# Nine double pairs of a SwiGLU feed-forward layer: a second split for product 3, a ring of four weights, four raw places, and moved X sums

## The chip, the cores and the metric

The kernel runs on one core of one Trainium2 chip. The metric is the device time of one execution in microseconds, the median of several runs. Smaller is better. A second number is the span of one profiled execution, from its first to its last recorded instruction, which the profile's shares refer to.

## The reference, cut to what matters

One decoder layer for 1032 tokens (a prompt of 1024 and 8 samples), in float32 with D_MODEL = 1024 and D_FF = 2816:

```python
def swiglu(x, wi, wo):
    g, u = jnp.split(x @ wi, 2, axis=-1)
    return (jax.nn.silu(g) * u) @ wo
...
    x = layer_norm(ALPHA * x + 0.5 * swiglu(x, ffn1_wi, ffn1_wo), ln_g[0], ln_b[0])
    z = x @ w_in + b_in
...
    x = layer_norm(ALPHA * x + mix, ln_g[1], ln_b[1])
    x = layer_norm(ALPHA * x + 0.5 * swiglu(x, ffn2_wi, ffn2_wo), ln_g[2], ln_b[2])
```

Between the two feed-forward layers stand an mLSTM branch and a short convolution branch, which the change does not touch. What it touches is `x @ wi` of both feed-forward layers: a product of the 1032 x 1024 activations with the gate and the up weights, 1024 x 2816 each.

## The kernel before, in words

**Precision.** Every float32 operand is split into a high part (a rounded copy in the format that the PE multiplies, "fp32r") and a low part (the difference). ACT makes the high part with a cast, DVE the low part with a subtraction. `product` (L490) issues three matmuls for each 128-row chunk: high weight by high X (L493), high weight by low X (L494), low weight by high X (L495).

**Pairs.** The 2816 gate columns and the 2816 up columns are cut into 11 pairs of 256, numbered 0 to 10. A pair's gate product (half k=0) and its up product (half k=1) are each a 2 x 2 block product of weights (two halves of K, two column blocks of 128) and X (two halves of K, two halves of 516 tokens). It is done with seven half products instead of eight, the scheme of Strassen and Winograd, numbered 0 to 6. A half product is done for two token pieces of 256 and 260 columns (`BN`), four K chunks and three matmuls each: 12 matmuls for a piece. Pair 0 is done plainly in `plain`, pair 1 with `hidden` and `pair` (L499), pairs 2 to 10 with `pair2` (L545), once gate and up together. These nine are the **double pairs**.

**The second split.** Product 1 of the gate half and product 1 of the up half multiply the same X block, so that together they are again a 2 x 2 block product: two weights, two halves of their K, two token pieces. `pair2` does them with seven quarter products of six matmuls, each 260 columns wide: 42 matmuls in place of 48. Their seven X operands `XQ` are made once for each feed-forward layer by `quarters` (L245), from the X blocks b11, b21, b12, b22 of product 1: ten sums on POOL, six on DVE, eight splits into high and low, and two small copies. The generator is advanced by the `beside` list: `pair` pops an entry after each step. The weights for quarters come from `wquarter` (L277): it packs two quarter weights into one slot.

**Weights.** For each pair and half, `wi_raw` (L677) issues two loads of 512 KB from the SP queue into two of three raw places (`raws`, 2 x 512 rows by 256 columns, named a30, a31, a32 in the first feed-forward layer), in rotation. `wcomb` (L306) forms the seven weights of a half: sums s1 and s2 on DVE, s3 and s4 on POOL, in `raw` tiles (a pool of 3), and then each weight's high and low part in a slot of the **ring**: nine tiles w0 to w5, e0, e1, cd, less one that `quarters` occupies (`qslots[2]`, w5), eight in all. A slot is free again when the last matmul on its weight is done.

**Results.** A half's products gather in PSUM tiles: `mm` (4 buffers), `aux` (3) and `pn` (1). ACT copies intermediate states into the snapshot tile (`sreg`, views `SN`), DVE adds the later ones to them; the gate passes through Silu on ACT and is multiplied with the up half on DVE (L569, L631). `spill` (L658) then forms the sums that the second weight matrix needs (L669, L671 on DVE, two on POOL) and stores them to `hsum` by nine transfers on the SP queue. The four `tmp` buffers, shared by `quarters`, by the up half and by `spill`, are free when their store has landed.

**What sets the order.** A scheduler lists each engine's instructions, by the order of the code, by data, by free buffers, and by `tc.high_priority()` and `tc.issue_after(...)`. Each engine then runs its list in order, so that an instruction that waits holds back all that stand behind it on the same engine. After the last double pair come the segments, the products with `wo`.

Each feed-forward layer runs one after the other: the first from the start to about 640 us, with the double pairs from 106 us, the second from about 1820 us, with its double pairs from about 1926 us.

## Time and profile before

| | |
|---|---|
| runs, us | 2669.59, 2673.85, 2673.53 |
| median, us | 2673.53 |
| profiled execution, its own time, us | 2669.52 |
| its span, us | 2667.2 |
| granted TensorE clock, mean | 0.997 |
| PE busy, us | 2622.7 |
| DVE busy, us | 1936.0 |
| ACT busy, us | 1293.1 |
| POOL busy, us | 696.0 |

The profile's page gives, for one profiled execution, the busy time of each engine, the chain of work that ended last, and groups of instructions. The trace behind it answers closer questions: busy time in stretches of the span (windows), what an engine waited for (waits), and single instructions with start and duration (timeline). An instruction of the timeline has its start in us, its duration, engine, line and operands; in brackets stands the idle time ahead of it and what ended it. A matmul's recorded duration overlaps that of the next, so its price is the distance from one start to the next.

### The profile page before, as it was taken

What the parts mean: (1) busy time and instruction counts of PE and PEld (TensorE: products, weight loads), DVE (VectorE), ACT (ScalarE), POOL (GpSimd) and SP (SyncE); (2) the same over time, 40 slices, a digit from 0 to 9 for tenths busy, and PEclk for the clock granted to TensorE, in tenths of its full rate; (3) what the DMA queues carried; (4) which work ended last, traced back from release to release, by engine and by line L of the source; (5) the groups of instructions that cost most, each with busy time, mean ns of one, the idle gap of its engine ahead of it and who ended that gap; (6) DMA issues with size and microseconds to landing.
All of it is one profiled execution on the core that took longest, in us unless ns stands there. A gap on an engine that the chain in (4) does not pass through costs nothing.

```text
span 2667.2 us, 56283 instructions
## 1 busy us (share of the span) xinstructions
PE 2622.7 (98%) x21660; PEld 2581.9 (97%) x21660; DVE 1936.0 (73%) x4272; ACT 1293.1 (48%) x2873; POOL 696.0 (26%) x705
## 2 busy tenths in 40 slices
PE   9999999999999999999999999999999999999998
PEld 9999999999999999999999999999999999999888
DVE  6867667987886656555555678668966666988787
ACT  5544446433654445446656555425544444543451
POOL 2422221112421111111110336323432222111454
PEclk9999999999999999999999999999999999999999
DMA  6232335532233434236667676812233324643211
GB/s 209 84 112 88 108 104 194 188 118 73 86 112 104 124 100 128 80 98 197 193 194 249 215 238 218 273 54 86 94 108 107 105 88 131 224 149 111 79 49 56
DMA packets 311924, 355.14 MB, mean 133 GB/s; under 512 B 28536, under 2 KB 246344, under 8 KB 311656
## 3 DMA queue, kind: packets, MB, share of 16 engines
q1 hardware_dynamic: 289336, 330.30, 39.0%
q10 hardware_dynamic: 22320, 21.26, 2.7%
q8 instruction: 169, 2.77, 0.4%
q14 instruction: 99, 0.81, 0.1%
HBM read 246.09 MB, written 105.42 MB: 132 GB/s over the span
## 4 chain that ended last, share of the span: by engine, by line
PE 87%; DVE 7%; DMA 2%; issue 2%; ACT 1%; POOL 1%; SPq 0%; DVEq 0%; ACTq 0%; POOLq 0%
PE mm L493 15%; PE mm L495 15%; PE mm L494 15%; PE mm L172 6%; PE aux L493 6%; PE mm L174 6%; PE mm L173 6%; PE aux L494 5%; PE aux L495 5%; PE pn L174 1%; PE pn L172 1%; PE pn L173 1%; DVE a L756 1%; DVE a L216 1%; PE pn L493 1%
## 5 line engine op out<-in xcount | busy, mean ns | idle before, releaser
L493 PE MATMUL mm<-a,w 128*128 128x260 f32 (+1 forms) x2511 | 712.8, 284 | 3.7 <-DVE a L779 3.1
L494 PE MATMUL mm<-a,w 128*128 128x260 f32 (+1 forms) x2511 | 706.5, 282 | 0.1
L495 PE MATMUL mm<-a,w 128*128 128x260 f32 (+1 forms) x2511 | 706.1, 282 | 0.0
L493 PEld LDWEIGHTS mm<-a,w 128*128 128x128 f32 x2511 | 473.7, 189 | 13.3 <-issue 8.0
L494 PEld LDWEIGHTS mm<-a,w 128*128 128x128 f32 x2511 | 474.0, 189 | 0.3 <-DVE a L216 0.3
L495 PEld LDWEIGHTS mm<-a,w 128*128 128x128 f32 x2511 | 473.2, 189 | 0.9 <-issue 0.8
L336 POOL TENSOR_TENSOR raw<-a,raw 128x512 f32<-128x512 f32 (+2 forms) x98 | 130.2, 1328 | 1026.7 <-DVE w L316 449.2
L316 DVE TENSOR_TENSOR w<-raw,w 128x512 fp32r<-128x512 f32 (+2 forms) x273 | 186.6, 684 | 126.9 <-ACT w L315 125.7
L493 PE MATMUL aux<-a,w 128*128 128x256 f32 (+1 forms) x760 | 215.4, 283 | 0.9 <-DVE a L515 0.7
L494 PE MATMUL aux<-a,w 128*128 128x256 f32 (+1 forms) x760 | 214.2, 282 | 1.8 <-DVE a L216 1.8
L315 ACT CAST w<-raw 128x512 fp32r<-128x512 f32 (+2 forms) x273 | 161.1, 591 | 111.6 <-PE mm L495 63.6
L174 PE MATMUL mm<-a,w 128*128 128x256 f32 (+4 forms) x758 | 214.6, 286 | 0.0
L495 PE MATMUL aux<-a,w 128*128 128x256 f32 (+1 forms) x760 | 213.6, 281 | 0.0
L172 PE MATMUL mm<-a,w 128*128 128x260 f32 (+3 forms) x712 | 204.6, 288 | 3.4 <-ACT w L1488 2.0
L173 PE MATMUL mm<-a,w 128*128 128x260 f32 (+3 forms) x712 | 202.7, 286 | 0.0
L493 PE MATMUL mm<-a,e 128*128 128x260 f32 (+1 forms) x629 | 178.7, 284 | 1.8 <-ACT sreg L511 0.8
L494 PE MATMUL mm<-a,e 128*128 128x260 f32 (+1 forms) x629 | 177.1, 281 | 0.0
L495 PE MATMUL mm<-a,e 128*128 128x260 f32 (+1 forms) x629 | 176.9, 281 | 0.0
L315 ACT CAST w<-a 128x512 fp32r<-128x512 f32 (+2 forms) x176 | 102.8, 586 | 147.9 <-PE mm L495 56.0
L326 POOL TENSOR_TENSOR raw<-a 128x512 f32<-128x512 f32 (+2 forms) x98 | 124.6, 1271 | 174.4 <-DVE w L316 80.0
L493 PEld LDWEIGHTS aux<-a,w 128*128 128x128 f32 x760 | 143.1, 188 | 3.5 <-issue 2.1
L494 PEld LDWEIGHTS aux<-a,w 128*128 128x128 f32 x760 | 143.1, 188 | 2.2 <-DVE a L216 2.2
(574 smaller groups left out, 7946.4 us busy)
## 6 DMA issues: line engine op xcount, KB each, us to landing
a<-in_ffn_wi_dram SPq DMA_DIRECT2D x80, 512.0 KB
a<-in_w_in_dram SPq DMA_DIRECT2D x68, 512.0 KB
a<-hsum SPq DMA_DIRECT2D x119, 258.0 KB
hsum<-a SPq DMA_DIRECT2D x68, 258.0 KB
a<-in_ffn_wo_dram SPq DMA_DIRECT2D x40, 384.0 KB
a<-in_state_C_dram ACTq DMA_DIRECT2D x32, 256.0 KB
out_dram<-a ACTq DMA_DIRECT2D x32, 256.0 KB
raw<-in_w_b_dram SPq DMA_DIRECT2D x32, 256.0 KB
```

The lines of the kernel that those rows point to most:

```text
L172: T.matmul(ps, wh, xh, start=(i == 0), stop=False)
L173: T.matmul(ps, wh, xl, start=False, stop=False)
L174: last = T.matmul(ps, wl, xh, start=False, stop=(i == n - 1))
L216: order_["lo"] = V.tensor_tensor(dst[1], src, F_(dst[0]), op=OP.subtract).ins
L315: S.copy(hi, src)
L316: V.tensor_tensor(lo, src, F_(hi), op=OP.subtract)
L326: G.tensor_tensor(s3, a11, a21, op=OP.subtract)
L336: G.tensor_tensor(s4, a12, s2, op=OP.subtract)
L493: T.matmul(ps, wh, xh, start=start and kp == 0, stop=False, skip_group_check=True)
L494: T.matmul(ps, wh, xl, start=False, stop=False, skip_group_check=True)
L495: T.matmul(ps, wl, xh, start=False, stop=stop and kp == len(xs) - 1, skip_group_check=True)
L756: V.tensor_tensor(lo, F_(lo), F_(hi), op=OP.subtract)
```

## The change

It has five parts.

1. **Product 3 is done by the second split too**, from pair 3 on (`LEVEL2 = {2: 1, 3: 3}`: product 1 from pair 2, as before, product 3 from pair 3). That is 42 matmuls in place of 48 in eight double pairs of each feed-forward layer. The seven quarter weights of product 3 come from the other half of the weights' columns; each pair makes seven more quarter weights, and two weights of 512 columns less.
2. **The X operands of product 3** are made by a second run of `quarters`, beside the first half of pair 3, into the tiles w4, e0 and e1. The X sums of product 1, which before stood beside the up half of pair 1, now stand beside the first half of pair 2.
3. **The ring has four slots** from pair 3 on: w0 to w3. At pair 2 it has eight. cd becomes a raw place.
4. **Four raw places**: each of a pair's four loads has its own place (`raws[:3] + ["cd"]`) in place of three in rotation. Some sums are now written in place into a raw tile (s3 over a21, s4 over s2).
5. **`pair2` is written anew** around `wcomb2`, a generator that yields the gate weights and then the up weights, in the order in which they are used: `first` and `second` are the steps of the gate and the up half, and the quarters of product 1 and then those of product 3 stand between the steps of the second half. Their results are added to the gate and up states with high priority.

In the core of the diff below, the lines left out are the old forms of `wquarter`, `wcomb` and `pair2`, and steps of `first` and `second` that read as those of the old `step`.

```diff
...
+    def use_ring(slots):
+        set_ring([i for i in from_ring() if i in slots])
...
-    def quarters(XS, slots):
-
-        (b11, b21), (b12, b22) = XS[0][9], XS[1][9]
+    def quarters(XS, j, slots):
...
+    def wcomb2(ra, rb, js):
...
+        def blocks(r):
+            return [u[:, :, i:i + 128] for u in r for i in (0, 128)]
+
+        def sums(r):
+            a11, a21, a12, a22 = blocks(r)
+            s1, s2 = k4(fresh()), k4(fresh())
+            V.tensor_tensor(s1, a21, a22, op=OP.add)
+            G.tensor_tensor(a21, a11, a21, op=OP.subtract)
+            V.tensor_tensor(s2, s1, a11, op=OP.subtract)
+            return s1, s2, a21
+
+        def last(r, s2):
+            G.tensor_tensor(s2, blocks(r)[2], s2, op=OP.subtract)
+            return s2
+
+        def quarter(i):
+            a11, a12, a21, a22 = (u[1][:, k:k + 2, i:i + 128] for u in (ra, rb) for k in (0, 2))
+            out = {1: put2(a12)}
+            yield out
+            out[0] = put2(a11)
+            yield
+            s1, s2 = (t.rearrange("p (k n) -> p k n", n=128) for t in fresh().rearrange("p (a m) -> a p m", a=2))
+            V.tensor_tensor(s1, a21, a22, op=OP.add)
+            V.tensor_tensor(s2, s1, a11, op=OP.subtract)
+            out[4] = put2(s1)
+            out[2] = put2(s2)
+            s3, s4 = (t.rearrange("p (k n) -> p k n", n=128) for t in fresh().rearrange("p (a m) -> a p m", a=2))
+            G.tensor_tensor(s3, a11, a21, op=OP.subtract)
+            G.tensor_tensor(s4, a12, s2, op=OP.subtract)
+            yield
+            out[3] = put2(a22)
+            out[5] = put2(s3)
+            yield
+            out[6] = put2(s4)
+            yield
+
+        wa, wb = {}, {}
+        s1, s2, s3 = sums(ra)
+        wa[0] = put(blocks(ra)[0])
+        wa[2] = put(s2)
+        if 3 not in js:
+            wa[3] = put(blocks(ra)[3])
+        wa[4] = put(s1)
+        s4 = last(ra, s2)
+        wa[5] = put(s3)
+        wa[6] = put(s4)
+        yield wa
+        wb[0] = put(blocks(rb)[0])
+        q = quarter(0)
+        wb[1] = next(q)
+        next(q)
+        next(q)
+        s1, s2, s3 = sums(rb)
+        wb[2] = put(s2)
+        next(q)
+        next(q)
+        if 3 in js:
+            q = quarter(128)
+            wb[3] = next(q)
+            next(q)
+            wb[4] = put(s1)
+            next(q)
+            next(q)
+            next(q)
+        else:
+            half.clear()
+            wb[3] = put(blocks(rb)[3])
+            wb[4] = put(s1)
+        s4 = last(rb, s2)
+        wb[5] = put(s3)
+        wb[6] = put(s4)
+        yield wb
+
...
+    def pair2(ws, XS, XQ, da, fa, fb):
 
...
-        for k, w in enumerate(ws):
-            P = {}
+        def quarter(ps, w, j, start, stop, x):
+            product(ps, w[j], [(x[j][:, 2 * k], x[j][:, 2 * k + 1]) for k in range(2)], start, stop)
+
+        def part(ps, d):
+            return ps[:, 0:d.shape[1]]
+
+        def add(d, ps, op=OP.add):
+            with tc.high_priority():
+                V.tensor_tensor(d, d, part(ps, d), op=op)
+
+        def minus(d, ps):
+            with tc.high_priority():
+                V.scalar_tensor_tensor(d, d, -1.0, part(ps, d), op0=OP.mult, op1=OP.add)
+
+        P = {}
+
...
+        add(g0, F)
+        add(g0, A)
+        add(u1, E)
+        fa(0, 0)
+        second(2, 0, w)
+        quarter(A, q, 2, False, False, x)
+        G_ = aux(BM)
+        quarter(G_, q, 3, True, True, x)
+        add(g1, A)
+        add(u0, G_, OP.subtract)
+        second(2, 1, w)
+        quarter(A, q, 5, False, True, x)
+        quarter(E, q, 6, False, True, x)
+        add(u0, A)
+        add(u1, A)
+        add(g1, E)
+        fa(0, 1)
+        for s, u in ((0, u0), (1, u1)):
+            fb(0, s, u)
+        if 3 in XQ:
+            q, x = w[3], XQ[3]
+            h0, h1 = (bs(da[1], s, BLK4) for s in range(2))
+            v0, v1 = (SN["v"][2][s] for s in range(2))
+            F, A = aux(BM), aux(BM)
+            quarter(F, q, 1, True, True, x)
+            quarter(A, q, 0, True, False, x)
+            add(h0, F, OP.subtract)
+            add(h0, A, OP.subtract)
+            fa(1, 0)
+            second(4, 0, w)
+            E = psp.tile([128, 512], F32, name="pn", tag="pn", bufs=1)[:, :BM]
+            quarter(E, q, 4, True, False, x)
+            S.copy(v1, E)
+            quarter(A, q, 2, False, False, x)
+            add(h1, A, OP.subtract)
+            G_ = aux(BM)
+            quarter(G_, q, 3, True, True, x)
+            S.copy(v0, part(G_, v0))
+            second(4, 1, w)
...
+    LEVEL2 = {2: 1, 3: 3}
...
         def wi_raw(p, k):
             i = 4 * p + 2 * k
-            return wraw(wi, k * FF + p * 256, [raws[(i + q + 2) % 3] for q in range(2)])
+            return wraw(wi, k * FF + p * 256, [(raws[:3] + ["cd"])[2 * k + q] if p > 2 else raws[(i + q + 2) % 3]
+                                               for q in range(2)])
 
...
-        set_ring([i for i in r if i != qslots[2]])
         wr = wi_raw(1, 0)
         with tc.issue_after(order_["entered"]) if l else nullcontext():
             w0 = wcomb(wr)
             xlate()
         for k in range(2):
-            if k:
-                late = quarters(XS, qslots)
-                beside.extend([[] for _ in range(5)])
-                XQ = next(late)
-                beside.extend([partial(next, late)] for _ in range(2))
             hidden(k, wcomb(wi_raw(1, k)) if k else w0, sg, k == 0)
         spill(1, sg)
+        XQ = {}
         for p in range(2, NHID // 2):
             sg = [gen(sgs[i]) for i in ((2, 1) if p % 2 == 0 else (0, 1))]
-            ra = wi_raw(p, 0)
-            wa_ = wcomb(ra, True)
-            rb = wi_raw(p, 1)
-            pair2([wa_, wcomb(rb, ra[1])], XS, XQ, sg)
+            if p in LEVEL2:
+                j = LEVEL2[p]
+                late = quarters(XS, j, qslots[j])
+                XQ[j] = next(late)
+                beside.extend([[partial(next, late)], [], [partial(next, late)]])
+                use_ring([i for i in ring["slots"] if i not in qslots[j] and (j == 1 or i != "cd")])
+
+            def gate(i, c):
+                d = bs(sg[i], c, BLK4)
+                S.activation(d, d, AF.Silu)
+
+            def up(i, c, t):
+                d = bs(sg[i], c, BLK4)
+                V.scalar_tensor_tensor(d, d, 0.5, t, op0=OP.mult, op1=OP.mult)
+
+            pair2(wcomb2(wi_raw(p, 0), wi_raw(p, 1), tuple(XQ)), XS, XQ, sg, gate, up)
             spill(p, sg)
-        r = ring["slots"][ring["i"] % 8:] + ring["slots"][:ring["i"] % 8]
-        set_ring([qslots[2]] + r)
+        set_ring([i for i in sum(qslots.values(), ()) if i in RING] + ["cd"] + from_ring())
...
 
     ffn(I["ffn1_wi"][0], I["ffn1_wo"][0], 0, X1, enter1, xlate1, [30, 31, 32, 33], [14, 15, 34, 35],
-        [16, 17, 24, 25, 18, 19, 20, 21], xscr, G1, T1, tail1, (33, 35, "w5"), [28, 29, 33])
+        [16, 17, 24, 25, 18, 19, 20, 21], xscr, G1, T1, tail1, {1: (33, 35, "w5"), 3: ("w4", "e0", "e1")}, [28, 29, 33])
 
 
...
```

**The order on PE at the start of pair 2** (the first feed-forward layer). In a row stand the line, the operation, the output, the operands and the tile; `mm`, `aux` and `pn` are PSUM tiles, the weight is the last name. Before, the last half product of pair 1 reads e1, and pair 2 begins with a quarter weight out of cd, ahead of its product 0 out of w4:

```order
L494 MATMUL aux_1672<-a23_1016,e1_1536 128x260
L495 MATMUL aux_1672<-a23_1016,e1_1536 128x260
L493 MATMUL aux_1802<-a5_142,cd_1559 128x260
L494 MATMUL aux_1802<-a5_142,cd_1559 128x260
L493 MATMUL mm_1604<-a0_139,w4_1524 128x256
L494 MATMUL mm_1604<-a0_139,w4_1524 128x256
L495 MATMUL mm_1604<-a0_139,w4_1524 128x256
L493 MATMUL mm_1604<-a0_139,w4_1524 128x256
L494 MATMUL mm_1604<-a0_139,w4_1524 128x256
L495 MATMUL mm_1604<-a0_139,w4_1524 128x256
```

In the changed kernel pair 2 begins with product 0 out of cd (`product` stands at L566 to L568 there):

```order
L568 MATMUL mm_1369<-a29_544,w3_1238 128x260
L566 MATMUL mm_1369<-a29_544,w3_1238 128x260
L567 MATMUL mm_1369<-a29_544,w3_1238 128x260
L568 MATMUL mm_1369<-a29_544,w3_1238 128x260
L566 MATMUL mm_1560<-a0_139,cd_1493 128x256
L567 MATMUL mm_1560<-a0_139,cd_1493 128x256
L568 MATMUL mm_1560<-a0_139,cd_1493 128x256
L566 MATMUL mm_1560<-a0_139,cd_1493 128x256
L567 MATMUL mm_1560<-a0_139,cd_1493 128x256
L568 MATMUL mm_1560<-a0_139,cd_1493 128x256
```

The quarter of product 1 is no longer the first work of pair 2: it stands in its second half, 168 matmuls later or more.

**The order on DVE in the second half of a double pair** (pair 5 and then the weights of pair 6). L316 and L291 are low parts in the kernel before, L325 and L295 weight sums, L556 adds of quarters, L591 and L592 reads of product 5. Before:

```order
L556 TENSOR_TENSOR sreg_830<-sreg_830,aux_3351 128x256
L556 TENSOR_TENSOR sreg_830<-sreg_830,aux_3351 128x260
L631 SCALAR_TENSOR_TENSOR a14_3060<-a14_3060,sreg_830 128x256
L316 TENSOR_TENSOR e0_3589<-raw_3584,e0_3589 128x512
L631 SCALAR_TENSOR_TENSOR a14_3060<-a14_3060,sreg_830 128x260
L295 TENSOR_TENSOR raw_3613<-a32_3608 128x256
L297 TENSOR_TENSOR raw_3613<-raw_3613,a30_3578 128x256
L316 TENSOR_TENSOR w1_3600<-raw_3585,w1_3600 128x512
L316 TENSOR_TENSOR w2_3603<-raw_3598,w2_3603 128x512
L591 SCALAR_TENSOR_TENSOR tmp_3496<-sreg_830,mm_3316 128x256
L592 TENSOR_TENSOR tmp_3499<-sreg_830,mm_3316 128x256
L325 TENSOR_TENSOR raw_3637<-a31_3606,a32_3608 128x512
```

In the changed kernel L286 is a low part, L631 the add of a quarter, L894 the product of gate and up, L316 and L318 weight sums of the next pair (a30 and a31 are raw places), and the reads of product 5 (L697) stand nine rows further down:

```order
L631 TENSOR_TENSOR sreg_830<-sreg_830,aux_3391 128x256
L631 TENSOR_TENSOR sreg_830<-sreg_830,aux_3391 128x260
L631 TENSOR_TENSOR a15_3124<-a15_3124,aux_3475 128x256
L286 TENSOR_TENSOR w3_3202<-raw_3197,w3_3202 128x256
L894 SCALAR_TENSOR_TENSOR a14_3123<-a14_3123,sreg_830 128x256
L286 TENSOR_TENSOR w3_3202<-cd_3131,w3_3202 128x256
L894 SCALAR_TENSOR_TENSOR a14_3123<-a14_3123,sreg_830 128x260
L286 TENSOR_TENSOR w0_3210<-raw_3205,w0_3210 128x256 x2
L286 TENSOR_TENSOR w1_3216<-a32_3129,w1_3216 128x512
L316 TENSOR_TENSOR raw_3658<-a30_3650,a31_3652 128x512
L631 TENSOR_TENSOR a15_3124<-a15_3124,aux_3475 128x260
L318 TENSOR_TENSOR raw_3659<-raw_3658,a30_3650 128x512
```

Before, between the adds of the last quarters of product 1 (output sreg) and the reads of product 5 (L591) stood two products of gate and up and five steps of weights (low parts and sums). Now there stand between them two products of gate and up, five adds of the quarters of product 3, and thirteen steps of weights, among them the first sum of the next pair (L316), which needs the raw place a31 loaded anew.

235 lines of the change are left out of this document (121 added, 114 removed).

## The prediction

> **What bounds the kernel now.** I read the page first: its head, the engines' busy times, and the chain that ended last.
>
> ```profile
> span 2667.2 us, 56283 instructions
> PE 2622.7 (98%) x21660; PEld 2581.9 (97%) x21660; DVE 1936.0 (73%) x4272; ACT 1293.1 (48%) x2873; POOL 696.0 (26%) x705
> ...
> PE 87%; DVE 7%; DMA 2%; issue 2%; ACT 1%; POOL 1%; SPq 0%; DVEq 0%; ACTq 0%; POOLq 0%
> L493 PE MATMUL mm<-a,w 128*128 128x260 f32 (+1 forms) x2511 | 712.8, 284 | 3.7 <-DVE a L779 3.1
> ```
>
> PE is idle for 2667.2 − 2622.7 = 44.5 us only. Fewer matmuls shorten the kernel, unless something else becomes late. The recorded 284 ns is no price, since matmuls overlap. The price comes from windows of one double pair each (columns: length; busy us and count of PE, PEld, DVE, ACT, POOL; granted clock; DMA share; GB/s).
>
> ```profile
> 138.70:177.92 39.22, 39.22 (x332) 39.22 (x331) 26.48 (x58) 17.60 (x44) 10.95 (x10) 1.00 0.33 102
> 217.14:256.38 39.24, 39.24 (x332) 39.24 (x332) 26.45 (x58) 17.73 (x44) 11.00 (x10) 1.00 0.34 102
> ```
>
> PE never stops here. A double pair has 330 matmuls: two halves of 6 half products (144 each) and 42 of the quarters; the other two records are cut by the edges. So one costs 39.23/330 = 0.119 us. DVE has 39.2 − 26.5 = 12.7 us free in each pair.
>
> The second place is the border between pairs 1 and 2. First the waits of PE over the whole kernel (total us, times, longest), then three windows in each feed-forward layer, then the timeline.
>
> ```profile
> PE aux L493 <- ACT cd L290: 4.5, 2, 2.3
> ```
>
> ```profile
> 100.00:105.00 5.00, 5.00 (x44) 5.00 (x44) 4.96 (x7) 1.12 (x3) 3.64 (x4) 1.00 0.00 0
> 105.00:110.00 5.00, 2.69 (x16) 2.39 (x15) 5.00 (x14) 2.83 (x9) 0.87 (x1) 0.83 0.00 0
> 110.00:115.00 5.00, 5.00 (x38) 5.00 (x37) 4.97 (x15) 1.51 (x5) 1.20 (x2) 0.83 0.61 191
> ```
>
> ```profile
> 1920.00:1925.00 5.00, 5.00 (x44) 5.00 (x43) 4.97 (x8) 1.30 (x3) 3.72 (x4) 1.00 0.00 0
> 1925.00:1930.00 5.00, 2.84 (x13) 2.33 (x13) 5.00 (x15) 2.38 (x7) 0.02 (x1) 0.76 0.01 3
> 1930.00:1935.00 5.00, 5.00 (x40) 5.00 (x39) 4.97 (x12) 1.36 (x4) 2.22 (x3) 0.90 0.76 246
> ```
>
> ```profile
> 105.88 0.28 PE L495 MATMUL aux<-a,e 128*128 128x260 f32 x1
> 108.46 0.58 PE L493 MATMUL aux<-a,cd 128*128 128x260 f32 x1 [2.31 <-ACT cd L290]
> ...
> 109.66 0.42 PE L495 MATMUL mm<-a,w 128*128 128x256 f32 x1
> 109.87 0.41 PE L493 MATMUL mm<-a,w 128*128 128x256 f32 x1
> ...
> 111.78 0.28 PE L495 MATMUL aux<-a,cd 128*128 128x260 f32 x1
> ```
>
> DVE is full there, PE waits 2.31 us for a quarter weight, and afterwards matmuls start 0.21 us apart (109.66, 109.87) until 111.78, at a granted clock of 0.83. The loss: the start at 108.46 is 2.58 us after the one before, 2.46 too much; the 14 matmuls that PE's order has up to 111.78 take 3.32 us in place of 14 x 0.119 = 1.67, 1.65 too much. Together 4.1 us. The second layer has about the same counts (13 + 40 against 16 + 38) and lost about 4.2 us.
>
> **Part by part.**
>
> *Matmuls.* Eight pairs in each layer do 42 in place of 48. In columns: a double pair before has 144 x 256 + 144 x 260 + 42 x 260 = 85,224, so 39.23 us / 85,224 = 0.460 ns a column; 24 x 516 columns become 42 x 260, 1,464 fewer, 0.67 us. Sixteen pairs: **−10.8 us**, on the path.
>
> *The border of pairs 1 and 2.* What filled DVE there were the X sums of product 1. They go into pair 2, and so does the quarter weight that PE waited for, 168 matmuls (20 us) later. I expect nothing in the place of this wait: product 0 needs one weight. **−8.3 us** for both layers.
>
> *X sums in pairs 2 and 3.* A set is 16 DVE and 10 POOL operations. Prices from the timeline, a steady pair first, then a stretch with X sums beside POOL:
>
> ```profile
> 182.17 0.41 DVE L592 TENSOR_TENSOR tmp<-sreg,mm 128x256 f32<-128x256 f32 x1
> 182.50 0.69 DVE L325 TENSOR_TENSOR raw<-a,a 128x512 f32<-128x512 f32 x1
> 183.10 0.75 DVE L569 SCALAR_TENSOR_TENSOR a<-a,tmp 128x256 f32<-128x256 f32 x2
> ...
> 98.82 0.97 DVE L216 TENSOR_TENSOR a<-tmp,a 128x260 fp32r<-128x260 f32 x1
> 99.72 0.42 DVE L295 TENSOR_TENSOR raw<-a 128x256 f32<-128x256 f32 x1
> 100.06 1.23 DVE L316 TENSOR_TENSOR w<-raw,w 128x512 fp32r<-128x512 f32 x1
> ```
>
> ```profile
> 97.68 1.83 POOL L257 TENSOR_TENSOR tmp<-a 128x260 f32<-128x260 f32 x2
> 99.88 0.86 POOL L257 TENSOR_TENSOR tmp<-a 128x260 f32<-128x260 f32 x1 [0.37 <-DVE a L216]
> ```
>
> From start to start a small DVE operation (256 or 260) takes 0.33 us and one of 512 takes 0.60. One that runs into a POOL operation takes 0.55 more (0.97 for 0.42, 1.23 for 0.69). A set costs DVE 16 x 0.33 = 5.3 us, and up to 10 x 0.55 = 5.5 more. Pair 2 then has 26.5 + 5.3 to 10.8 = 32 to 37 us of DVE work in 39.2: it fits by the sum, but its sums wait for the four `tmp` buffers, which the stores of pair 1 hold:
>
> ```profile
> 193.49 0.43 DVE L671 TENSOR_TENSOR tmp<-a,tmp 128x260 f32<-128x260 f32 x1 [2.26 <-DMA hsum<-tmp]
> ```
>
> Pair 3 has 30.4 (next part) + 5.3 to 10.8 = 36 to 41 us in 38.6: a stall of 0 to 2.6 us. I take 1.0 for pair 2 (0 to 2.3, the wait above) and 1.5 for pair 3: **+5.0 us** in both layers, 0 to 10.
>
> The Trainium skill, "SBUF — State Buffer", Who interferes with whom, says that a DVE instruction with two SBUF inputs and a GpSimd instruction that reads SBUF exclude each other, and that the second one waits for the whole first one. The trace agrees in kind (0.55 us more, beside POOL operations of 0.86 to 0.92). By the rule at its worst a set would cost 10 x 0.9 = 9 us more on DVE, not 5.5, and pair 3 would stall for up to 6 us.
>
> *Steady pairs 4 to 10.* DVE does, for each pair, 54 small and 14 large operations in place of 41 and 16: 13 x 0.33 − 2 x 0.60 = +3.1 us, and POOL two more quarter sums, up to 2 x 0.55 on DVE: +3.9 with part of it, 26.5 to about 30.4 us in a period of 39.23 − 0.67 = 38.56, 79%. ACT has 39.2 − 17.7 = 21.5 us free and gains a few casts. So averages hide it; the order decides. The tightest stretch is the second half of a pair. From the end of product 1's quarter 6 to the first matmul of the next pair's product 4, which writes the PSUM buffer of this pair's product 4, PE has 145 matmuls = 17.2 us (145 x 0.119). In its list DVE has in that time 26 small (8.6) and 8 large (4.8) operations up to the read of that buffer (L702): 13.4 us, some three collisions, 1.7 us, and two waits: for the last quarter 5, and for the load of a31, whose place the weight of quarter 6 frees only in this half. The load's price, in windows of 1 us after its issue at 235.58:
>
> ```profile
> 235.58 0.38 SPq L273 DMA_DIRECT2D a<-in_ffn_wi_dram  x1
> ```
>
> ```profile
> 236.50:237.50 1.00, 1.00 (x11) 1.00 (x10) 0.22 (x1) 0.87 (x2) 0.00 (x0) 1.00 0.71 169
> 237.50:238.50 1.00, 1.00 (x11) 1.00 (x10) 0.87 (x3) 0.02 (x1) 0.00 (x0) 1.00 1.00 337
> 238.50:239.50 1.00, 1.00 (x10) 1.00 (x10) 0.36 (x3) 0.75 (x3) 0.00 (x0) 1.00 0.06 18
> ```
>
> It lands about 3 us after the issue; I place the issue 2.9 us into this stretch, so it lands at 6.0, when DVE comes to it at 5.7. With 1.5 us for both waits DVE needs 13.4 + 1.7 + 1.5 = 16.6 us of 17.2. It just fits. Cost **0**, with 0 to 1.5 us a pair as bounds, from the longer landing in the chain that ended last:
>
> ```profile
> 1854.32 4.60 DMA a<-in_ffn_wi_dram
> ```
>
> *Ring of four.* Low and high parts are released at least 1.5 us before they are needed by my count of matmuls; covered by the same DVE list, so not counted again.
>
> *Last double pair to segments.* DVE is denser there; 0 to 3 us a layer, nearest to the small waits that PE has now: **+2 us**.
>
> Sum: 2669.5 (the profiled execution) − 10.8 − 8.3 + 5.0 + 2.0 = 2657.4 us, −12.1. The profiled execution is the low one of the runs shown (2669.59, 2673.85, 2673.53); on the median the sum gives 2673.5 − 12.1 = **2661.4**.
>
> A new gap may cost more than itself: the 2.31 us gap brought 1.65 us of slow matmuls. The Trainium skill, "TensorE: Matmul & The Clock Gate", What's actually happening, lets the clock fall to half after an idle window of about 3.4 us. Here 2.31 us were enough (clock 0.83). If pairs 2 and 3 each had such a gap, four would cost 4 x 4.1 = 16.4 us by the rows, and 4 x 2.46 = 9.8 if by that rule the clock stayed.
>
> **The rivals.**
>
> *A, all of it is hidden:* no stall in pairs 2 and 3 nor at the end; −19.1, 2654. For it speaks that DVE has time to spare by the sum; against it the full windows whenever X sums run.
>
> *D, the X sums' stall only moves:* two gaps like the old one in each layer's pairs 2 and 3, less 40%: +10 in place of +5; −7.1, 2666.4. For it speaks that pair 3 has more DVE work than time.
>
> *C, the steady gain is eaten:* DVE overruns the 17.2 us by 0.67 us in each of 14 pairs: +9.4; −2.7, 2670.8, no change.
>
> *B, slower:* the same list in the second half of each double pair, with the load of a31 landing 1.5 us later and two more collisions (1.1 us): 16.6 + 2.6 = 19.2, 2.0 over, of which I let 1.4 stay (between 0.67, case C, and 2.0). 14 x 1.4 = +19.6, so +7.5, 2681. It takes the whole gain from 0.86 us a pair (12.1 / 14) and shows as slower from 1.24 ((12.1 + 5.3) / 14). For it: the margin is 0.6 us and the load is late by construction. Against it: DVE is only 79% busy, and hsum stores, the other traffic on SP's queue, come later.
>
> **How the numbers follow.** No change means within 0.2%, 5.3 us, about what a measurement of this kernel can tell. Forecast 0.44, A 0.12, D 0.15, C 0.14, B 0.15. Faster: forecast and A, and about two thirds of D: 0.66; same: the rest of D and C: 0.20; slower: 0.14. The range goes from 2652 (A, with its 2 us) to 2677, leaving out most of B and the edge of A.
>
> **What would show it.** A period of 38.5 to 38.6 us in pairs 4 to 10 with PE idle near 0 and DVE at about 30 us; windows at 105 to 115 and 1925 to 1935 full at clock 1.00; gaps of 1 to 2.5 us in pair 2 or 3. Periods above 39.2 with PE waiting for DVE at product 0 or 4 of the next pair would be B, periods near 39.2 would be C, and gaps with a lowered clock in pairs 2 and 3 would be D.

## The result, and the profile after

| | before | changed |
|---|---|---|
| runs, us | 2669.59 to 2673.85, median 2673.12 (4) | 2695.03, 2698.34, 2698.99 |
| ratio | | 1.0094 (95%: 1.0080 to 1.0109) |
| span of the profiled execution, us | 2667.2 | 2693.4 |
| PE busy, us | 2622.7 | 2625.2 |

The change made the kernel about 25 us slower, where 12 us faster was forecast. A fourth execution of the changed kernel had a granted clock of 0.835 throughout and took 2857.63 us; it is left out, and the profile below is one of a later execution of the same kernel (the first run of the experiments).

The page of the changed kernel, its head and the busy times:

```profile
span 2693.4 us, 56531 instructions
PE 2625.2 (97%) x21564; PEld 2573.7 (96%) x21564; DVE 2032.4 (75%) x4480; ACT 1311.8 (49%) x2969; POOL 744.5 (28%) x757
```

The 96 matmuls are gone (21660 to 21564). PE is now idle for 68.2 us, not 44.5. Its busy time did not fall either; a recorded matmul (0.28 us) overlaps the next, which starts 0.119 us later, so short delays count as busy, but how much of the 2.5 us more this is was not worked out. So the matmuls were saved, and more than that was lost. Where? The first sum of `spill` marks a pair's end. These are its starts on DVE for pairs 1 to 4, before (L669) and changed (L812), from the timelines:

```profile
113.30 0.42 DVE L669 TENSOR_TENSOR tmp<-a 128x256 f32<-128x256 f32 x1
148.17 0.42 DVE L669 TENSOR_TENSOR tmp<-a 128x256 f32<-128x256 f32 x1
187.48 0.42 DVE L669 TENSOR_TENSOR tmp<-a 128x256 f32<-128x256 f32 x1
226.62 0.42 DVE L669 TENSOR_TENSOR tmp<-a 128x256 f32<-128x256 f32 x1
```

```profile
106.70 0.41 DVE L812 TENSOR_TENSOR tmp<-a 128x256 f32<-128x256 f32 x1
148.51 0.41 DVE L812 TENSOR_TENSOR tmp<-a 128x256 f32<-128x256 f32 x1
195.98 0.41 DVE L812 TENSOR_TENSOR tmp<-a 128x256 f32<-128x256 f32 x1
234.26 0.41 DVE L812 TENSOR_TENSOR tmp<-a 128x256 f32<-128x256 f32 x1
```

Without the 4.1 us of the old gap, pair 2 would have ended at 144.1; it ended at 148.5, **4.4 us** late. Pair 3 took 47.47 us, and 38.56 were to be expected: **8.9 us**. Pair 4 took 38.28. The same periods in the second layer: 42.48, 46.19 and 38.66. These marks stand on DVE, which in pair 3 falls behind PE. A second measure goes by PE alone: how much later the changed kernel starts a matmul than the kernel before starts the same one (counted from the start in both traces, one profiled execution each, with six taken off for each pair in which product 3 is split):

| the moment in the kernel before, us | PE's lag, us |
|---|---|
| 105.00, pair 1 | −1.3 |
| 113.30, mark of pair 1 | −5.4 |
| 148.17, pair 2 | −0.5 |
| 187.48, pair 3 | 5.4 |
| 383.53, pair 8 | 4.4 |
| 480.00, the segments run | 12.2 |
| 1920.00, second layer, pair 1 | 16.1 |
| 1932.22, mark of pair 1 | 12.0 |
| 1967.22, pair 2 | 17.3 |
| 2006.52, pair 3 | 22.0 |
| 2242.28, pair 9 | 22.4 |
| 2300.00, the segments run | 26.7 |

A pair that is split should make the lag 0.67 us smaller. By this measure pairs 2 and 3 lose 4.9 and 6.6 us in the first layer, 5.4 and 5.3 in the second, 22.2 us in all. And there is a third place, which the marks do not reach: between pair 8 of the first layer and its segments 9.1 us are lost, between pair 9 of the second and its segments 4.9. The steady pairs in between lose 6.8 us together.

The pairs behind pair 4 have windows like these, one pair each:

```profile
273.38:312.54 39.16, 38.98 (x327) 38.65 (x326) 31.51 (x70) 18.51 (x48) 13.45 (x12) 1.00 0.32 103
312.54:351.89 39.35, 38.94 (x327) 38.61 (x325) 31.43 (x69) 18.62 (x48) 13.45 (x12) 1.00 0.33 102
351.89:391.31 39.42, 38.80 (x327) 38.63 (x326) 32.32 (x69) 18.61 (x48) 12.51 (x12) 1.00 0.32 101
```

39.2 to 39.4 us in place of 38.56: the saved 0.67 us is eaten in each pair. The old gap itself is gone in both layers, as forecast. In windows of 5 us PE is full at clock 1.00 where it was busy for 2.69 and 2.84 of 5 us (the second layer comes later now, and its pair 2 begins at 1938.34):

```profile
105.00:110.00 5.00, 5.00 (x45) 5.00 (x44) 4.07 (x12) 1.36 (x4) 2.80 (x2) 1.00 0.57 165
...
1935.00:1940.00 5.00, 5.00 (x45) 5.00 (x44) 4.92 (x9) 1.41 (x4) 2.72 (x3) 1.00 0.01 2
```

What DVE waits for in six steady pairs of the first layer (200 to 450 us), and PE in the three pairs above (total us, times, longest):

```profile
DVE w L286 <- ACT w L285: 21.2, 25, 3.0
DVE tmp L814 <- DMA hsum<-tmp: 10.1, 6, 2.5
DVE raw L316 <- DMA a<-in_ffn_wi_dram: 5.4, 6, 1.2
```

```profile
PE mm L566 <- DVE tmp L702: 1.2, 3, 0.6
```

The third row is the load of a31, 0.9 us in each pair, and the row of PE is the next pair's product 4: the place that the prediction named. The first two rows are longer, but they stay much as they are (17.8 and 11.5 us) in the run with seven raw places below, where PE waits for nothing. In pair 3 the windows show something else, DVE itself (pairs 2, 3 and 4, from mark to mark):

```profile
106.70:148.51 41.81, 38.27 (x312) 37.23 (x311) 31.86 (x66) 16.64 (x43) 18.63 (x19) 1.00 0.31 99
148.51:195.98 47.47, 42.95 (x346) 41.34 (x345) 42.56 (x85) 22.53 (x59) 20.77 (x22) 1.00 0.26 78
195.98:234.26 38.28, 38.05 (x321) 37.87 (x321) 30.33 (x69) 18.17 (x48) 12.91 (x12) 1.00 0.33 112
```

In pair 3 DVE is busy for 42.56 us, more than the pair's matmuls take, and idle for 4.9. In pair 2 it is not full. There it waits, behind the stores of pair 1 (timeline of DVE, ACT and PE):

```profile
112.01 0.43 DVE L814 TENSOR_TENSOR tmp<-a,tmp 128x260 f32<-128x260 f32 x1 [2.94 <-DMA hsum<-tmp]
113.44 0.37 ACT L651 COPY a<-aux 128x256 f32<-128x256 f32 x1 [5.29 <-POOL tmp L815]
114.36 1.00 DVE L286 TENSOR_TENSOR w<-raw,w 128x512 fp32r<-128x512 f32 x1 [1.92 <-ACT w L285]
121.02 0.39 PE L566 MATMUL mm<-a,w 128*128 128x256 f32 x1 [1.81 <-DVE a L631]
123.36 0.39 PE L566 MATMUL mm<-a,w 128*128 128x260 f32 x1 [0.68 <-DVE a L631]
```

`first` copies the gate's states into the state tile that the pair before used too (one of the two tiles of `sg` is shared by all pairs). The copy at L651 therefore waits for POOL's sum at L815, this one for DVE's at L814 (and, by POOL's own row, for a store too), and DVE's for a `tmp` buffer, which a store holds. ACT stands still for 5.29 us, and with it the casts of the weights behind the copy. That this chain sets the time of pair 2 is a reading of the timeline; the second run under "Without X sums" tests it, and it does not hold alone.

The third place is the end of the double pairs. The last double pairs and their segments, before and changed (first layer), and the longest wait of PE there:

```profile
433.00:480.00 47.00, 46.87 (x395) 46.70 (x394) 40.41 (x86) 34.26 (x67) 7.21 (x6) 1.00 0.85 303
455.00:470.00 15.00, 15.00 (x129) 15.00 (x128) 15.00 (x36) 13.68 (x27) 1.36 (x1) 1.00 1.05 392
```

```profile
441.00:490.00 49.00, 44.41 (x346) 42.85 (x345) 44.40 (x98) 35.43 (x72) 8.75 (x7) 0.97 0.77 271
475.00:485.00 10.00, 7.71 (x49) 7.21 (x50) 10.00 (x21) 3.01 (x4) 1.03 (x1) 0.83 0.39 124
478.25 0.39 PE L566 MATMUL mm<-a,cd 128*128 128x256 f32 x1 [2.27 <-DVE tmp L702]
```

Before, PE is full there, but so is DVE, for 15 us on end. Changed, 346 matmuls, which at 0.119 us are 41.2, take 49 us: DVE is full again, PE waits 2.27 us for its read of product 6 (L702), and the clock is 0.83 around it.

### The profile page after: what moved, and what is told of

The parts are those of the page before. It is cut to its first block, busy times and chain, and to the rows that moved or that the text cites. A ratio compares the mean times of both kernels' runs of the same rounds, so it can differ in the third digit from the quotient of the medians.

```text
span 2855.9 us, 56531 instructions
## 1 busy us (share of the span) xinstructions
PE 2822.8 (99%) x21564; PEld 2778.4 (97%) x21564; DVE 2032.9 (71%) x4480; ACT 1321.0 (46%) x2969; POOL 731.1 (26%) x757
## 5 line engine op out<-in xcount | busy, mean ns | idle before, releaser
L566 PE MATMUL mm<-a,w 128*128 128x260 f32 (+1 forms) x2755 | 820.5, 299 | 7.2 <-ACT w L285 3.1
L567 PE MATMUL mm<-a,w 128*128 128x260 f32 (+1 forms) x2755 | 815.9, 297 | 1.0 <-DVE a L223 1.0
L568 PE MATMUL mm<-a,w 128*128 128x260 f32 (+1 forms) x2755 | 808.4, 297 | 1.1 <-DVE w L286 1.1
L566 PEld LDWEIGHTS mm<-a,w 128*128 128x128 f32 x2755 | 547.5, 199 | 17.5 <-issue 10.0
L567 PEld LDWEIGHTS mm<-a,w 128*128 128x128 f32 x2755 | 548.1, 199 | 1.4 <-DVE a L223 1.4
L568 PEld LDWEIGHTS mm<-a,w 128*128 128x128 f32 x2755 | 543.6, 199 | 2.4 <-DVE w L286 1.3
L409 POOL TENSOR_TENSOR raw<-a,raw 128x512 f32<-128x512 f32 (+2 forms) x62 | 77.6, 1251 | 802.6 <-issue 352.9
L566 PE MATMUL aux<-a,w 128*128 128x260 f32 (+1 forms) x864 | 256.8, 297 | 1.2 <-DVE sreg L631 0.6
L567 PE MATMUL aux<-a,w 128*128 128x260 f32 (+1 forms) x864 | 255.2, 296 | 0.0
L568 PE MATMUL aux<-a,w 128*128 128x260 f32 (+1 forms) x864 | 253.9, 295 | 0.0
L179 PE MATMUL mm<-a,w 128*128 128x256 f32 (+3 forms) x702 | 210.0, 300 | 1.6 <-DVE a L963 0.8
L180 PE MATMUL mm<-a,w 128*128 128x256 f32 (+3 forms) x702 | 208.9, 299 | 0.0
L181 PE MATMUL mm<-a,w 128*128 128x256 f32 (+3 forms) x702 | 207.3, 298 | 0.0
L566 PEld LDWEIGHTS aux<-a,w 128*128 128x128 f32 x864 | 170.0, 197 | 4.5 <-issue 2.3
L567 PEld LDWEIGHTS aux<-a,w 128*128 128x128 f32 x864 | 170.4, 197 | 0.3 <-DVE a L223 0.3
L568 PEld LDWEIGHTS aux<-a,w 128*128 128x128 f32 x864 | 169.4, 196 | 0.0
L393 DVE TENSOR_TENSOR w<-raw,w 128x512 fp32r<-128x512 f32 (+2 forms) x160 | 104.7, 654 | 82.3 <-ACT w L392 82.0
L286 DVE TENSOR_TENSOR w<-raw,w 128x256 fp32r<-128x256 f32 (+1 forms) x234 | 128.1, 559 | 41.4 <-ACT w L285 40.7
L285 ACT CAST w<-raw 128x256 fp32r<-128x256 f32 (+1 forms) x234 | 114.2, 500 | 84.2 <-PE mm L568 51.7
L566 PE MATMUL mm<-a,e 128*128 128x256 f32 (+1 forms) x501 | 148.2, 296 | 0.3 <-DVE a L928 0.3
L567 PE MATMUL mm<-a,e 128*128 128x256 f32 (+1 forms) x501 | 146.9, 293 | 0.0
L568 PE MATMUL mm<-a,e 128*128 128x256 f32 (+1 forms) x501 | 146.7, 293 | 0.0
```

The lines of the kernel that those rows point to most:

```text
L179: T.matmul(ps, wh, xh, start=(i == 0), stop=False)
L180: T.matmul(ps, wh, xl, start=False, stop=False)
L181: last = T.matmul(ps, wl, xh, start=False, stop=(i == n - 1))
L285: S.copy(dst[0], src)
L286: V.tensor_tensor(dst[1], src, F_(dst[0]), op=OP.subtract)
L393: V.tensor_tensor(lo, src, F_(hi), op=OP.subtract)
```

## The experiments

Two theories at first. **S**, steady: the list of DVE overruns in each of pairs 4 to 10. **B**, borders: the loss lies in pairs 2 and 3 and at the ends of the double pairs.

**The changed kernel once more** (no edit).

> The changed kernel once more, for a profile at full clock. Theory S (steady): DVE's list in the second half of each double pair overruns, and each of the pairs 4 to 10 pays for it; what is missing against my sum is 25.5 + 12.1 = 37.6 us, over 14 pairs 2.7 us each, so their period is 38.56 + 2.7 = 41.2 us and PE is seen waiting for DVE or for the ring once in each pair. Theory B (borders): the period is 38.6 us with no wait, and the 37 us lie in gaps of several us with a lowered clock in pairs 2 and 3 and at the change to the segments, in both feed-forward layers. Time 2699 by both.

2696.19 us, ratio 1.0103 (1.0083 to 1.0123). Neither theory alone: the periods are 39.2, not 41.2 and not 38.6, and pairs 2 and 3 lose 13 us in each layer by DVE's marks (11 by PE's lag). All experiments below are compared with this run.

**Product 3 not split.** Three variants of the rest of the change, with `LEVEL2` cut:

```diff
-    LEVEL2 = {2: 1, 3: 3}
+    LEVEL2 = {2: 1}
```

The first has the old raw places and ring besides (`raws[(i + q + 2) % 3]`, eight slots), the second four raw places and a ring of seven, the third four raw places and w0 to w3 alone.

> Product 3 is not split: ring of eight and three raw places as before, only the rewritten order and the X sums of product 1 in pair 2 stay. Theory S: the period is 39.2 us, the gap between pairs 1 and 2 is gone (-8.3 us), a wait of 1 us stays in pair 2: 2673 - 8.3 + 2 = 2667 us. Theory B: pair 2 has a gap of 4 us or more in each layer, and the end of the double pairs as well: 2673 to 2685 us.

> As the one without the split of product 3, but with four raw places from pair 3 on, cd among them, and so a ring of seven. Theory S with the ring as its cause: seven slots are enough, within 2 us of the run with eight. If the late loads were the cause (one place for each of a pair's loads): up to 2.7 us a pair, 38 us more than that run.

> As the one without the split of product 3, but with four raw places and a ring of only four slots (w0 to w3) from pair 3 on; w4, e0 and e1 stay unused in the double pairs. Theory S with the ring as its cause: 2.7 us a pair, period about 42 us, some 38 us above the run with eight slots. Theory S with the added DVE work of the split as its cause: period 39.2, within 3 us of the run with eight slots. Theory B: like the run with eight slots.

2705.50 (1.0111 to 1.0149), 2678.58 (1.0017 to 1.0039) and 2677.24 us (1.0017 to 1.0035). The first was a miss by both theories, and the two others, which were forecast beside it, missed with it. It told most: with three raw places in rotation the rewritten order loses some 27 us against four, though product 3 is not split. The waits of DVE for loads in six of its steady pairs say why:

```profile
DVE raw L332 <- DMA a<-in_ffn_wi_dram: 10.0, 6, 2.9
...
DVE raw L316 <- DMA a<-in_ffn_wi_dram: 5.9, 6, 2.2
```

The ring of four costs nothing: the third variant has steady pairs as before, with PE full (pairs 3 and 4):

```profile
149.57:188.80 39.23, 39.23 (x332) 39.23 (x332) 27.57 (x59) 17.79 (x44) 10.92 (x10) 1.00 0.31 102
188.80:228.03 39.23, 39.23 (x332) 39.23 (x332) 27.59 (x58) 17.78 (x44) 10.90 (x10) 1.00 0.33 102
```

It is still 6 us slower than before, without any split of product 3 and without the old gap: its pair 2 takes 41.39 us, with X sums of product 1 (by PE's lag it loses 5.0 and 4.5 us in the two layers). At the end of the first layer's double pairs it loses 0.4 us, and the second variant 0.8, where the changed kernel loses 9.1.

**Without X sums, and with the gate's states elsewhere.** Theory X: the X sums fill DVE and POOL in pairs 2 and 3. Theory W: ACT's wait for the pair before costs the time. The first run leaves out all X sums of products 1 and 3 (the quarters multiply blocks that are there already). The second keeps them, and copies the states of products 3 and 4 into the snapshot tile, as the kernel before did:

```diff
-                S.copy(e0, ps)
+                S.copy(SN["v"][2][s], ps)
...
-                S.copy(e1, P["E", s])
+                S.copy(SN["v"][3][s], P["E", s])
```

> The changed kernel without the X sums of products 1 and 3 (twenty POOL, twelve DVE operations and sixteen splits in each feed-forward layer are left out, the quarters read blocks that are there already). Theory X, the X sums themselves fill DVE and POOL in pairs 2 and 3: nearly all of the 14 us that each layer loses there goes, 2697 - 25 = 2672 us or less. Theory W, ACT is held back there by a wait for the sums of the pair before (the copy of L655 into the state tile that those sums still read), and the X sums only fill what time is left: less than half of it goes, 2685 us or more. In pairs 4 to 10 nothing changes by both (39.2 us).

> The changed kernel, with the gate's intermediate states of products 3 and 4 copied into the snapshot tile, as before the change, and no longer into the state tile that the pair before still reads. Theory W: ACT's waits for the POOL sum of L815 go (2 to 5 us in each pair), pairs 2 and 3 lose less than half of their 14 us in each layer: 2697 - 14 to 20 = 2677 to 2683 us. Theory X: within 4 us of 2697.

2679.06 (1.0019 to 1.0044), between the two forecasts, and 2700.22 us (1.0091 to 1.0131), as theory X said. The X sums cost 17 us of 25. Theory W falls for the changed kernel: with the copies out of the way pair 2 takes 41.78 us, as before 41.81. ACT's wait for the sums of pair 1 is gone there, and DVE waits for a POOL sum of the X operands instead (L265), after which PE stops for 1.64 us where it stopped for 1.81 in the changed kernel:

```profile
119.42 0.43 DVE L266 TENSOR_TENSOR tmp<-tmp 128x260 f32<-128x260 f32 x1 [3.27 <-POOL tmp L265]
122.13 0.39 PE L566 MATMUL mm<-a,w 128*128 128x256 f32 x1 [1.64 <-DVE a L666]
```

Pair 3 takes 46.36 us there, with DVE at 42.79, as full as in the changed kernel. Without X sums pair 3 takes 40.80 us, with DVE at 32.34:

```profile
147.07:187.87 40.80, 40.46 (x341) 40.29 (x340) 32.34 (x70) 19.43 (x50) 12.11 (x12) 1.00 0.30 97
```

So a set of X sums costs DVE 42.56 − 32.34 = 10.2 us, the upper end of what the prediction worked out (5.3 to 10.8). What it took too low was the rest: 32.3, not 30.4.

**X sums of product 1 beside pair 1 again**, without and with the states in the snapshot tile.

```diff
+            if k:
+                late = quarters(XS, 1, qslots[1])
+                beside.extend([[] for _ in range(5)])
+                XQ[1] = next(late)
+                beside.extend([partial(next, late)] for _ in range(2))
             hidden(k, wcomb(wi_raw(1, k)) if k else w0, sg, k == 0)
```

> The changed kernel, with the X sums of product 1 put back beside the up half of pair 1, the ring there without w5. Theory X: pair 2 is free of stalls but the border of pairs 1 and 2 loses about 4 us in each layer, as before the change; about 2 us a layer better or worse, 2693 to 2701 us. Theory W: pair 2 still waits for the sums of pair 1, which now come later since DVE is full there: 2 to 4 us a layer worse, 2701 to 2705 us.

> The changed kernel, with the gate's states in the snapshot tile and the X sums of product 1 beside pair 1. If the two edits add up, theory W gives 2677 to 2685 us; theory X gives 2693 to 2701 us.

2702.21 (1.0099 to 1.0139) and 2698.53 us (1.0084 to 1.0124): 6 and 2 us above the changed kernel, with intervals that overlap its own. The time of the first run lies in the range of theory W, but not for its reason: pair 2 does not stall (34.22 us from mark to mark, 34.87 in the kernel before). The old gap comes back for the stall of pair 2, and pair 3 takes 49.78 and 48.25 us in the first layer.

**Seven raw places.** The late load measured by itself: the run without X sums, whose tiles w4, e0 and e1 stand empty, and take loads.

```diff
-(raws[:3] + ["cd"])[2 * k + q] if p > 2
+(raws[:3] + ["cd", "w4", "e0", "e1"])[(i + q) % 7] if p > 2
```

> The run without X sums (2679 us), and the three tiles that then stand empty (w4, e0, e1) used as three more raw places from pair 3 on, so that a load waits for a place of the pair before the last and not for the quarter weights of this one. Theory L, the late load of a31 holds DVE back in the second half of pairs 4 to 10 (0.9 us in each by the waits of DVE): the period goes from 39.2 to 38.6 us, 14 x 0.65 = 9 us less, 2670 us. Rival: the length of DVE's list does it, 31.5 us of busy time in a pair; the period stays at 39.1 to 39.3, 2677 to 2681 us.

2680.91 us (1.0027 to 1.0059): as a time a miss, but the periods answer. Windows of 38.50 us each, from pair 4 on:

```profile
199.00:237.50 38.50, 38.50 (x327) 38.50 (x326) 30.61 (x69) 18.64 (x48) 14.44 (x13) 1.00 0.32 102
237.50:276.00 38.50, 38.50 (x327) 38.50 (x326) 30.43 (x69) 18.65 (x48) 14.42 (x13) 1.00 0.34 105
```

The split does bring its 0.67 us a pair once the load is not late. DVE waits for no load any more, and PE for nothing; DVE's list is as long as before (69 instructions), so the length does not decide. (In the second layer the period is 38.65.) The time gained is lost again in pairs 2 and 3: pair 2 takes 43.65 us, 38.51 without these places. Its ring has the same three tiles, and DVE waits 4.7 us there for a load into e0 and e1. At the start of pair 3 PE waits 2.63 us for ACT's copy of the gate's state, which itself waited 6.07 us for POOL's sum of the pair before. So by this timeline theory W's wait does cost time here, without X sums.

**The X sums on DVE alone, and spread.** Theory C: collisions with POOL and the passing to and fro make the sums dear. Theory D: DVE is simply full in pair 3. The first run has `V.` for `G.` in the five sums of `quarters`. The second puts the sums of product 3 beside the end of pair 3 and the start of pair 4, and splits product 3 from pair 4 on. The third does both.

```diff
-                G.tensor_tensor(x, F_(b[:, h]), F_(b[:, l]), op=OP.add)
-            G.tensor_tensor(x4, x3, x2, op=OP.subtract)
+                V.tensor_tensor(x, F_(b[:, h]), F_(b[:, l]), op=OP.add)
+            V.tensor_tensor(x4, x3, x2, op=OP.subtract)
...
+                    beside.extend([[] for _ in range(12)] + [[partial(next, late)]])
...
+            if p == 4:
+                XQ[3] = xq
+                beside.extend([[], [partial(next, late)]])
```

> The changed kernel with all X sums of products 1 and 3 on DVE, none on POOL. Theory C, collisions with POOL and the passing to and fro make the sums dear: 26 DVE operations x 0.33 = 8.7 us in place of the 10.2 us that a set now costs DVE, and the waits between become shorter; pair 3 loses 2 to 4 us less, both layers 4 to 10 us less, 2687 to 2693 us. Rival, DVE's count of operations decides: 2 to 3 us a layer more, 2700 us or more.

> The changed kernel with the X sums of product 3 later and spread: one half beside the end of pair 3, one beside the start of pair 4, product 3 split from pair 4 on (two pairs fewer in all are split, +1.3 us). Theory D, DVE is simply full in pair 3 (42.6 us busy): the 8.9 us that pair 3 loses shrink to 2 to 4 us over pairs 3 and 4; 2697 + 1.3 - 10 to 14 = 2684 to 2688 us. Rival, the waits for tmp buffers and for the sums of the pair before cost the same wherever they stand: 2695 us or more.

> The spread X sums, and all of them on DVE. If theories C and D both hold, the gains add: 2678 to 2685 us. If only D holds, 2684 to 2688.

2690.23 (1.0063 to 1.0103), 2692.76 (1.0070 to 1.0110) and 2687.40 us (1.0048 to 1.0088). Against the 2696 of the changed kernel that is 6, 3 and 9 us less, with intervals that overlap its own. The first lies in the range of theory C, the second above that of theory D, and the third not in the range for added gains (2678 to 2685) but in that for D alone. The periods tell more. Pairs 2 to 4 of the first layer take 127.56 us in the changed kernel, and 125.18, 123.42 and 119.78 in these runs (second layer: 127.33, then 127.13, 124.15 and 121.17); there the gains add, and more. The spread runs give some of theirs back ahead of the second layer, where PE stands for 4.75 and 4.54 us at about 1850, which it does not in the changed kernel; why was not looked into. Pair 3 with all sums on DVE:

```profile
147.35:191.54 44.19, 42.91 (x353) 42.03 (x352) 41.42 (x95) 22.50 (x59) 14.71 (x12) 1.00 0.29 87
```

Ten more DVE instructions (95 for 85), and 1.1 us less of DVE time (41.42 for 42.56). Yet what pair 3 gains pair 4 loses: pairs 3 and 4 together take 85.75 us in the changed kernel, 85.90 with the sums on DVE, 81.98 when spread, and 81.04 with both. Putting the sums on DVE pays in pair 2, 39.28 us for 41.81, where DVE is not full. So theory C's part shows in pair 2, and theory D's in pairs 3 and 4.

**The last questions.** Why does pair 2 stall without X sums; why do the variants lose time between the two feed-forward layers, in code that is the same; and do collisions count in the kernel before too? The first run is the kernel before with the ring's slots in the changed order after the double pairs; then the run without X sums, and the spread one on DVE, with the gate's states in the snapshot tile; then the kernel before with its X sums on DVE.

```diff
-        set_ring([qslots[2]] + r)
+        set_ring([qslots[2], "w4", "e0", "e1", "cd"] + [i for i in r if i in RING[:4]])
```

> The kernel before, with one thing of the change: the order in which the ring hands out its nine slots after the double pairs (w5, w4, e0, e1, cd, then w0 to w3). If that order is why the variants lose 3 to 5 us between the two feed-forward layers, in code that the change does not touch: 2674 to 2677 us. If not: 2669 to 2673 us, like before.

> The run without X sums (2679 us), with the gate's states in the snapshot tile. Pair 2 loses about 3 us a layer there without any X sum, while ACT waits 5 us for the POOL sum of the pair before. If that wait of ACT is the cause, the loss goes: 2673 to 2675 us. If it is DVE's own wait for the tmp buffers: 2678 to 2682 us.

> Spread X sums on DVE (2687 us) and the gate's states in the snapshot tile. If the wait of ACT costs in pairs 2 to 10 once DVE is less full: 2678 to 2683 us. If not: 2686 to 2690 us.

> The kernel before, with its X sums all on DVE in place of DVE and POOL. If collisions are what fills DVE beside pair 1 (theory C), the gap at the border of pairs 1 and 2 shrinks by 1 to 3 us in each layer: 2665 to 2669 us. If DVE's count of operations decides, it grows: 2673 to 2677 us.

The order of the slots: 2674.20 us, 1.0020 (1.0010 to 1.0030). A list of nine names, cd before or behind w0 to w3, costs the kernel before about 4 us (2.7 to 8 by the interval), 3.3 of them between pair 8 of the first layer and pair 1 of the second (1551.96 us from mark to mark for 1548.69).

Without X sums and with the states moved: 2676.46 us (1.0011 to 1.0034), 2.6 us less than with the states unmoved, with intervals that overlap, and between the two forecasts. Pair 2 of the first layer still stalls, by another wait of ACT. In its list a cast for the later segments (L893) stands ahead of a copy out of PSUM, and waits for sums to come back from `hsum`:

```profile
118.55 0.62 ACT L893 CAST a<-a 128x516 fp32r<-128x516 f32 x1 [6.28 <-DMA a<-hsum]
119.81 0.39 PE L553 MATMUL mm<-a,w 128*128 128x260 f32 x1 [2.28 <-ACT sreg L642]
```

```profile
115.00:120.00 5.00, 2.72 (x23) 2.52 (x22) 1.52 (x3) 1.20 (x3) 0.44 (x1) 1.00 0.24 72
120.00:125.00 5.00, 5.00 (x30) 5.00 (x30) 3.62 (x9) 3.50 (x9) 0.00 (x0) 0.66 0.23 63
```

The spread sums with the states moved: 2687.58 us (1.0047 to 1.0082), no gain.

The kernel before with its X sums on DVE: **2666.25 us, 0.9984 (0.9974 to 0.9994)**, the only version that beats both. The gap at the border of pairs 1 and 2 shrinks from 2.31 to 0.8 us (and is another wait, for a PSUM buffer), and the clock stays at 1.00. Whether the collisions with POOL or the waits for its results were dear, this run does not tell apart:

```profile
PE mm L493 <- DVE tmp L531: 0.8, 1, 0.8
```

```profile
105.00:110.00 5.00, 4.20 (x36) 4.00 (x35) 5.00 (x13) 1.73 (x5) 0.56 (x1) 1.00 0.03 5
110.00:115.00 5.00, 5.00 (x45) 5.00 (x44) 4.71 (x12) 1.36 (x4) 2.39 (x3) 1.00 0.81 262
```

**Remedies in the changed kernel.** First the ring's order alone (`from_ring() + ["cd"]`), then this with spread sums on DVE and the states in the snapshot tile.

> The changed kernel with the ring's slots after the double pairs in the order of the kernel before (cd last). The same edit turned round cost the kernel before about 5 us; so 2697 - 3 to 5 = 2692 to 2694 us. If the order matters only with the rest of the kernel before as it was: 2695 to 2699 us.

> All remedies in the changed kernel: X sums on DVE and spread, the gate's states in the snapshot tile, the ring's order as before. What is left is the late load of a31 (9 us), some 3 us a layer in each of the pairs 2 and 3 to 4, and two pairs that are not split. 2680 to 2685 us, still slower than before; if the gains hang on each other, up to 2690.

2697.47 (1.0067 to 1.0105) and 2684.88 us (1.0031 to 1.0061). The first is not told apart from the changed kernel: what the order of slots costs there stays open. All together win back about 11 of 25 us. At the end of the first layer's double pairs, where the changed kernel loses 9.1 us by PE's lag, these two lose 9.5 and 7.7, and each of the runs above that split product 3 loses 5.7 to 9.9.

## Why the prediction was wrong

*Matmuls, −10.8 us: right.* With loads in time the period is 38.50, forecast 38.56.

*The border of pairs 1 and 2, −8.3 us: right.* Both gaps are gone, and nothing took their place at that point.

*X sums in pairs 2 and 3, +5.0 us, bounds 0 to 10: the first step that failed.* By PE's lag both pairs lost 11.5 us in the first layer and 10.7 in the second, some 22 us (by DVE's marks 13.3 and 12.7). The mechanism was in the text, rival D; its size was wrong for three reasons. The sum for pair 3 was 36 to 41 us of DVE work in 38.6, and the value was taken from the middle; it was 42.56. The sum had no place for idle time of DVE while work waits, 4.9 us in pair 3. And for pair 2 the bound of 2.3 us was the length of one wait; several follow one another there (DVE for a buffer 2.94 us, for ACT 1.92, for POOL's sums). That `first` now writes early into a tile that the pair before still reads stands in the diff, and it was not followed to ACT's queue; but moving these copies alone gained nothing, since the wait for POOL's X sum took their place.

*Steady pairs, 0, bounds 0 to 1.5: mis-sized, inside its bounds.* The prediction had the place (the load of a31, and PE at the next pair's product 4) and a margin of 0.6 us. It set the load at 3.0 us from issue to landing, level with DVE; DVE then waited 0.9 us for it. A load of the same place in a steady pair was issued at 296.47 and used at 300.05, 3.58 us later:

```profile
296.47 0.38 SPq L280 DMA_DIRECT2D a<-in_ffn_wi_dram  x1
```

```profile
300.05 0.69 DVE L316 TENSOR_TENSOR raw<-a,a 128x512 f32<-128x512 f32 x1 [0.76 <-DMA a<-in_ffn_wi_dram]
```

Pairs 4 to 8 of the first layer and 4 to 9 of the second took 195.33 and 236.01 us; 11 x 38.56 = 424.2, so 7.2 us were lost, 0.65 a pair (6.8 by PE's lag). That is rival C's size (0.67), and the run with seven places shows that it came from the late load. It came on top of D.

*Ring of four, no cost: right* in the variant with a ring of four, which does not split product 3; with the split it was not tried.

*Last double pair to segments, +2 us, bounds 0 to 3 a layer: the second step that failed.* It took 9.1 us in the first layer and 4.9 in the second, 14 in all (the last two double pairs of the first layer and the last of the second among them). The prediction saw that DVE is denser there, but it went by the small waits that PE had, and not by DVE's own time: in the kernel before DVE was already full for 15 us on end (455 to 470). The loss goes with the split: the two variants with four raw places that do not split product 3 lose 0.8 and 0.4 us in the first layer, −0.9 and 1.4 in the second. The ring's order is not the cause (9.5 us with the old order in the first layer). That DVE's time ran out there is argued from its full windows; which of the added instructions costs it stays open.

With these the account closes: −10.8 − 8.3 + 22.2 + 6.8 + 14.0 = +23.9 us of the 26.2 between the spans. Another 4.0 us were lost in the code between the layers, for which the prediction had no term, and 1.7 gained elsewhere. The order of the ring's slots can cost about 4 us there, shown in the kernel before only.

So no one rival was right. Each of C and D was priced with all else at its best, and their chances stood beside each other as if one excluded the other. Their sum is +9.4 + 22 − 19.1 = +12 us, on the other side, without the 14 at the end of the double pairs. The sign of being slower was given to B alone, and B's place, the steady pairs, was not where most of the time went.

## What to carry to other kernels

When an engine is to do 36 to 41 us of work in 38.6, take the upper end, and add the waits that its place in the order brings; a margin of 0.6 us beside a load that is late by construction is none. For each copy that is moved earlier, ask who still reads its target, and what stands behind it on its engine. Look at the end of a stretch too: where the next phase already fills the engine, in windows of the kernel before, added work has little room. Mechanisms that rest on the same engine add up: price them together before they are given separate chances.

## What the runs showed of the hardware

A gap of 2.28 us (the run without X sums, with the states moved) was followed by a window at a granted clock of 0.66 (30 matmuls in 5 us for 44), as the gap of 2.31 us before was; gaps of 1.81 and 0.68 us within three us were not (pair 2 of the changed kernel, where the clock of the 5 us around them is 1.00):

```profile
120.00:125.00 5.00, 3.29 (x25) 3.10 (x26) 5.00 (x13) 3.53 (x9) 2.85 (x4) 1.00 0.01 3
```

But the length of the gap does not decide it. The same wait, 1.79 us long, was followed by slow matmuls in the run with the ring of four (clock 0.80), and a wait of 3.55 us at 2550.67 in the kernel before was not (clock 1.00):

```profile
122.61 0.39 PE L566 MATMUL mm<-a,w 128*128 128x256 f32 x1 [1.79 <-DVE a L631]
120.00:125.00 5.00, 3.21 (x19) 2.97 (x19) 5.00 (x12) 3.12 (x9) 3.15 (x4) 0.80 0.00 0
```

```profile
2550.67 0.70 PE L468 MATMUL aux<-sreg,onesm 128*128 128x256 f32 x2 [3.55 <-DVE sreg L465]
2550.00:2555.00 5.00, 4.33 (x33) 4.22 (x34) 4.03 (x10) 1.65 (x4) 0.33 (x1) 1.00 0.01 2
```

So a wait of PE of about 2 us can cost more than itself in these runs (1.65 us more at the old gap, by the prediction's count), or not; what decides was not found. The Trainium skill, "TensorE: Matmul & The Clock Gate", What's actually happening, puts the idle window at about 3.4 us; these traces show shorter gaps that were enough (1.79, 2.28 and 2.31 us) and one of 3.55 us that was not.

Sums that POOL takes off DVE can cost DVE more than it would spend on them: with ten POOL sums a set cost 10.2 us of DVE time in pair 3, and with all of them on DVE 1.1 us less, for ten more instructions. The Trainium skill, "SBUF — State Buffer", Who interferes with whom, gives a reason, that such instructions of the two engines exclude each other; the trace agrees in kind (0.97 us for 0.42 beside a POOL operation, in the prediction's rows).
